# A two-layer decoder trunk: index scores of the sparse attention summed over the heads on TensorE with diagonal operands, in place of multiply-and-add steps on VectorE

## The chip, the cores and the metric

The kernel runs on one core of a Trainium2 chip. The metric is the device time of one execution in microseconds (us); the time before is the median of three runs. The profile is of one further execution, with its own time. TensorE (PE, with its weight loads PEld) multiplies matrices and writes only to PSUM; VectorE (DVE), ScalarE (ACT) and GpSimd (POOL) work elementwise; SyncE (SP) issues the DMAs here. Each engine takes its instructions in the order in which the program holds them.

## The reference

The model has two layers. Layer 0 runs two groups of heads in parallel on 256 tokens of width 1024: A, a sliding-window attention, and B, a sparse attention in which an indexer picks 64 keys per query. Layer 1 is a block attention. After each attention and each MLP stands a residual with a layer norm, and every step is modulated by factors from a conditioning vector `c` (the "ada" products). The change touches the indexer of B only:

```python
def one_block(args):
    i, qb, iqb, iwb = args                       # 128 queries, 8 index heads of 64
    raw = jnp.einsum('bqhd,bsd->bhqs', iqb, ik)  # index scores of each head
    score = jnp.einsum('bhqs,bqh->bqs', jax.nn.relu(raw), iwb)   # weighted sum over the 8 heads
    score = jnp.where(causal, score, -inf)
    _, idx = lax.top_k(score, 64)                # S // 4 keys of each query
    ...                                          # softmax attention over the picked keys
```

For each query the eight heads' scores pass through a ReLU, are multiplied by eight weights of that query (`iw`), and are added up. The largest 64 of the sum select the keys.

## The kernel before

The 256 tokens are two blocks of 128 (b = 0 and 1), tokens on the partitions. Block 0 sees 128 keys, block 1 sees 256. All is float32; large weight matrices are split by ACT (L170) and DVE (L171) into a high and a low part, and each product is three matmuls (L236 to L238).

The order of the program comes from a scheduler: code is emitted in an order written out by hand (the strings of steps at L887 and L954, generators that are advanced in turn), each instruction gets a priority from its place, shifted by a few tuned offsets (L46), and the scheduler sets the final order on each engine. Buffers are rings of tiles: `wh` and `wl` (six each) hold split weights, `q4`, `r2`, `prob` and so on the activations; PSUM has four rings (`a` to `d`) of two banks. Reuse of a ring's tile waits for the last reader of what it held.

The stage around the change, by the lines that the prediction names:

- L661 and L681 project the tokens; L715 copies the result `g0` out of PSUM. From it come the keys, the latent queries and the weights `iw` (L765). L736 to L741 normalise the latent queries: DVE sums the squares, POOL computes the power -1/2 (L302), DVE scales (L741), TensorE transposes (L744) and ACT copies (L746).
- L784 makes queries of them, a pair of matmuls for each of four query sets (index queries of both blocks, attention queries of both blocks). Each is rotated by DVE (L471 to L475, `rope`), transposed (L491) and copied by ACT (L493).
- `index(b)`: for each pair of heads, two matmuls of 128 queries by 128 or 256 keys (L817), one ReLU by ACT out of PSUM into `rl` (L819), and for each head one DVE instruction (L822) that multiplies by the head's weight of each query and adds to `score`; the first adds to the causal mask.
- `select(b)` then takes the largest eight (L833) and strikes them out (L834), eight times, and makes a mask (L837, L838).
- Beside this runs group A's attention in half steps: two score matmuls (L531), mask and maximum on DVE (L535), exponentials on ACT (L539), transposes (L545), products with the values (L553).
- Into each half step one "ada" product is placed on TensorE: eight matmuls on a loaded weight tile (L347), a copy by ACT (L357), two matmuls with one column (L368), and an addition on DVE (L377). A fixed chain holds these, L531, L545 and L553 in turn on TensorE. L347 needs a PSUM bank that an earlier L377 has read.
- SP loads the weights into a ring of four raw tiles (L164). A tile's successor is issued when its tile has been read.
- L410 and L417 spread a gate vector over the partitions; L608 uses it in the residual after the output projection (`ps_out`). Then follow the first MLP, layer 1 and the second MLP, which are nearly all dense matmuls.

Of the kernel before, what the change touches and what calls it, by code (L numbers as in the profile page):

```python
# [17 lines left out]
F32 = mybir.dt.float32  # L18
# [3 lines left out]
AF = mybir.ActivationFunctionType  # L22
ALU = mybir.AluOpType

P = 128
D = 1024
KT = 8
NB = 2
# [36 lines left out]
def trunk(ctx: ExitStack, tc, c, x, pos, small, ln, ada, w_g, w_g1, w_uq, w_out, c_in, c_out, w1, w2, out):  # L65
    nc = tc.nc
    const = ctx.enter_context(tc.tile_pool(name="const", bufs=1))
    wp = ctx.enter_context(tc.tile_pool(name="wp", bufs=NRAW))
    sp = ctx.enter_context(tc.tile_pool(name="sp", bufs=NSPLIT))
    hp = ctx.enter_context(tc.tile_pool(name="hp", bufs=1))  # L70
    work = ctx.enter_context(tc.tile_pool(name="work", bufs=1))
    psum = ctx.enter_context(tc.tile_pool(name="psum", bufs=1, space=bass.MemoryType.PSUM))

    def pa(name):
        return psum.tile([P, 512], F32, name=name, tag="a", bufs=2)

    def pb(name):
        return psum.tile([P, 512], F32, name=name, tag="b", bufs=2)

    def pc(name):  # L80
        return psum.tile([P, 512], F32, name=name, tag="c", bufs=2)
# [173 lines left out]
    for b in range(NB):  # L255
        t = const.tile([P, D], F32, name=f"x{b}")
# [10 lines left out]
    for h in range(2):  # L267
        ps = pa("ps_c")
# [7 lines left out]
    ident = const.tile([P, P], F32, name="ident")  # L276
# [335 lines left out]
    def moments(st):  # L612
        mv = col([P, 2], "mv")
        nc.vector.bn_aggr(mv, st.rearrange("p a s -> p (a s)"))
        rs = col([P, 1], "rs")
        nc.vector.tensor_scalar_add(rs, mv[:, 1:2], LN_EPS)
        rsqrt(rs, rs)
        return mv, rs
# [44 lines left out]
    for k in range(KT):  # L663
# [16 lines left out]
        for b in range(NB):  # L680
            nc.tensor.matmul(g1[b], hk[:, b * P:(b + 1) * P], parts["g1", k // 2][0][:, k % 2 * 512:k % 2 * 512 + 512],  # L681
                             start=k == 0, stop=k == KT - 1)
# [3 lines left out]
    m = nc.vector.tensor_copy(posf, posi)  # L686
# [40 lines left out]
    iw = work.tile([P, NB, 8], F32, name="iw")  # L727
# [4 lines left out]
    for b in range(NB):  # L732
        t = g0[b]
# [3 lines left out]
                                       op0=ALU.mult, op1=ALU.add, accum_out=ss)  # L737
# [4 lines left out]
        ps = pc("ps_cq")  # L742
# [5 lines left out]
    for b in range(NB):  # L748

        t = g0[b]  # L750
        q = slice(b * P, (b + 1) * P)
# [3 lines left out]
        ps = pc("ps_kd")  # L755
# [8 lines left out]
        nc.gpsimd.tensor_copy(vB[:, b, :64], t[:, 320:384])  # L764
        nc.vector.tensor_scalar_mul(iw[:, b], t[:, 448:456], IW_SCALE)  # L765

    def q4(name):
        return work.tile([P, 4, 256], F32, name=name, tag="q4", bufs=5)

    def to_qT(qf, dst, b):  # L770
# [3 lines left out]
             [(d[:, :, b * P:(b + 1) * P], slice(i * n, (i + 1) * n)) for i, d in enumerate(dst)])  # L774

    iqT, aqT = q4("iqT"), q4("aqT")
    bqT = work.tile([P, 1040], F32, name="bqT", tag="vv", bufs=2)[:, :1024].rearrange("p (n q) -> p n q", n=4)
    hf = lambda t: t.rearrange("p (h q) d -> p h q d", h=2)
# [28 lines left out]
    def index(b):  # L807
        nk = P * (b + 1)
        m = mC[:, P:] if b == 0 else mC
        sc = work.tile([P, 256], F32, name="score", tag="prob2", bufs=2)  # L810
        first = True
        for p0 in (0, 2):
            for half in range(2):
                ps = pb("ps_i")
                rl = work.tile([P, 2, 256], F32, name="rl", tag="prob", bufs=3)
                for j in range(2):
                    nc.tensor.matmul(ps[:, j * 256:j * 256 + nk], iqT[:, p0 + j, b * P:(b + 1) * P],  # L817
                                     ikT[half][:, :nk], start=True, stop=True)
                nc.scalar.activation(rl[:, :, :nk], ps.rearrange("p (j k) -> p j k", j=2)[:, :, :nk], AF.Relu)  # L819
                for j in range(2):  # L820
                    hd = 2 * (p0 + j) + half
                    nc.vector.scalar_tensor_tensor(sc[:, :nk], in0=rl[:, j, :nk], scalar=iw[:, b, hd:hd + 1],  # L822
                                                   in1=(m if first else sc[:, :nk]), op0=ALU.mult, op1=ALU.add)
                    first = False
        return sc

    def select(b, sc):
# [28 lines left out]
    def index_keys(b):  # L856
        scores[b] = index(b)
# [194 lines left out]
    def c_project(g, got):  # L1052
        qT = q4("cqT_")

        kT = [q4("ckT_"), work.tile([P, 4 + 2 * g, 256], F32, name="ckT_", tag=("pair", "keys")[g])[:, :4]]
        for half in range(2):
            nc.gpsimd.memset(kT[half][(1 - half) * HD:(2 - half) * HD], 0.0)
        vv = work.tile([P, 1040], F32, name="vv", tag="vv", bufs=2)
        vv = vv.rearrange("p (b h e) -> p b h e", b=NB, h=8)
        got += [qT, kT, vv]  # L1060
        nc.gpsimd.memset(vv[:, :, :, 64:], 1.0)

        def products(part, b):
            ps = pa("ps_c")
            project(ps, hT, b, [("ci", 6 * g + 2 * part), ("ci", 6 * g + 2 * part + 1)])
            if part == 2:
                nc.scalar.copy(vv[:, b, :, :64], heads_of(ps))
            else:
                b_rope(ps, ([qT], kT)[part], b)

        for part, b in ([(0, 0), (1, 0), (0, 1), (1, 1)] if g == 0 else [(0, 0), (0, 1), (1, 0), (1, 1)]) + [(2, 0), (2, 1)]:
            products(part, b)
            if b == 1:
                ahead(1)
            if g == 0 and (part, b) != (0, 0):
                for _ in range(2):
                    next(more, None)
            yield
# [33 lines left out]
    first = moments(zs[0][1])  # L1112
# [4 lines left out]
    for s in halves:  # L1117
        z = zs[1][0]
        nc.vector.scalar_tensor_tensor(z[:, s], in0=z[:, s], scalar=mv[:, 0:1], in1=gb[0][:, s],  # L1119
                                       op0=ALU.subtract, op1=ALU.mult)  # L1120
# [55 lines left out]
```

## Time and profile before

| | |
|---|---|
| median of three runs | 667.27 us (663.51 to 668.79) |
| profiled execution, its time | 670.48 us |
| its span, first to last instruction | 668.7 us |
| PE / DVE / ACT / POOL busy | 636.8 / 470.5 / 339.4 / 34.1 us |
| mean granted TensorE clock | 0.976 |
| L822, first and last start | 60.4 and 79.1 us |

The profile gives times from the start of the span. Where rows of one kind follow each other, a group stands as its first start, the time to its last end, and a count; a float32 matmul of 128 or 256 columns is recorded as two rows, so "x4" is two matmuls. Ends of matmuls are modelled, so the time that one costs is read from start to next start. In brackets stands how long an engine was idle before a row, and what ended that.

### The profile page before, as it was taken

The page shows a single profiled execution, that of the slowest core. Times are in us where ns is not written, and L with a number is a line of the kernel's source. Part 1 is how long each engine was busy: PE and PEld are TensorE (multiplying, and loading weights), DVE is VectorE, ACT ScalarE, POOL GpSimd, SP SyncE. Part 2 cuts the span into 40 slices and gives each one's busy share as a digit, 9 for nine tenths or more (in the row PEclk, how much of TensorE's full clock was granted, in tenths as well). Part 3 has the DMA queues.
Part 4 walks back from the last instruction along what each step waited for, and adds up shares of the span by engine and source line. Part 5 has one row for each costly group of instructions (what it writes and reads, how often), then busy time and mean ns, then how long its engine had stood idle before and what let it go on. Part 6 is the DMA issues. An engine that isn't in the chain of part 4 may idle for free. (4 is left out here: it accounts for less than half of the span.)

```text
span 668.7 us, 9851 instructions
## 1 busy us (share of the span) xinstructions
PE 636.8 (95%) x3802; PEld 533.1 (80%) x3802; DVE 470.5 (70%) x885; ACT 339.4 (51%) x540; POOL 34.1 (5%) x69
## 2 busy tenths in 40 slices
PE   6998998989999999999989999999999999999994
PEld 3554776868899998989867888888899989898983
DVE  2848987348778989888796996755867755554447
ACT  3325657436645445445544555873654554545440
POOL 5010000100010000200010000000000000000004
PEclk8999989989999999999979999999999999999997
DMA  8993879233679897899742486311467755565101
GB/s 305 409 414 114 298 272 350 95 126 125 239 270 368 328 370 272 330 362 370 273 179 101 159 356 223 137 72 63 143 235 256 296 204 190 197 235 195 67 1 63
DMA packets 24385, 151.52 MB, mean 227 GB/s; under 512 B 2833, under 2 KB 3089, under 8 KB 8338
## 3 DMA queue, kind: packets, MB, share of 16 engines
q1 hardware_dynamic: 24194, 150.71, 60.9%
q8 instruction: 30, 0.49, 0.3%
q10 hardware_dynamic: 144, 0.18, 0.1%
q14 instruction: 17, 0.14, 0.1%
HBM read 149.83 MB, written 1.05 MB: 226 GB/s over the span
## 5 line engine op out<-in xcount | busy, mean ns | idle before, releaser
L170 ACT CAST wh<-w_w 128x1024 fp32r<-128x1024 f32 x128 | 130.9, 1051 | 152.8 <-PE ps_m L237 66.6
L171 DVE TENSOR_TENSOR wl<-w_w,wh 128x1024 fp32r<-128x1024 f32 x128 | 153.4, 1222 | 70.5 <-ACT wh L170 70.3
L236 PE MATMUL ps_m<-hTh,wh 128*128 128x256 f32 x448 | 126.8, 283 | 0.0
L238 PE MATMUL ps_m<-hTh,wl 128*128 128x256 f32 x448 | 126.7, 283 | 0.0
L237 PE MATMUL ps_m<-hTl,wh 128*128 128x256 f32 x448 | 126.6, 283 | 0.0
L238 PE MATMUL ps_m<-wh,ul 128*128 128x512 f32 x256 | 101.4, 397 | 0.6 <-DVE ul L171 0.6
L236 PE MATMUL ps_m<-wh,uh 128*128 128x512 f32 x256 | 101.1, 398 | 0.0
L237 PE MATMUL ps_m<-wl,uh 128*128 128x512 f32 x256 | 100.8, 395 | 0.0
L322 DVE CUSTOM_DVE_ANT_0 junk<-w_ada,cB,sm 128x1024 bf16<-128x1024 f32 x68 | 87.1, 1282 | 15.1 <-DMA w_ada<-in_ada_dram 13.6
L237 PEld LDWEIGHTS ps_m<-hTl,wh 128*128 128x128 f32 x448 | 85.7, 191 | 1.3
L236 PEld LDWEIGHTS ps_m<-hTh,wh 128*128 128x128 f32 x448 | 85.7, 191 | 1.2
L238 PEld LDWEIGHTS ps_m<-hTh,wl 128*128 128x128 f32 x448 | 85.8, 191 | 0.0
L238 PEld LDWEIGHTS ps_m<-wh,ul 128*128 128x128 f32 x256 | 48.2, 188 | 12.2 <-DVE ul L171 1.2
L236 PEld LDWEIGHTS ps_m<-wh,uh 128*128 128x128 f32 x256 | 48.3, 189 | 10.2 <-ACT uh L170 0.6
L237 PEld LDWEIGHTS ps_m<-wl,uh 128*128 128x128 f32 x256 | 48.2, 188 | 9.7 <-DVE wl L171 0.2
L236 PE MATMUL ps_c<-wh,hTh 128*128 128x512 f32 x96 | 39.6, 416 | 2.8 <-ACT hTh L170 2.0
L237 PE MATMUL ps_c<-wl,hTh 128*128 128x512 f32 x96 | 39.0, 408 | 0.0
L238 PE MATMUL ps_c<-wh,hTl 128*128 128x512 f32 x96 | 38.6, 402 | 0.0
L171 DVE TENSOR_TENSOR ul<-relu,uh 128x512 fp32r<-128x512 f32 (+1 forms) x36 | 22.6, 627 | 17.5 <-ACT uh L170 17.5
L539 ACT ACTIVATE prob<-prob,negm 128x128 f32<-128x128 f32 (+1 forms) x64 | 26.8, 452 | 14.8 <-DVE negm L535 14.8
L171 DVE TENSOR_TENSOR wl<-w_ci,wh 128x1024 fp32r<-128x1024 f32 x24 | 28.6, 1213 | 5.3 <-ACT wh L170 5.2
L170 ACT CAST wh<-w_ci 128x1024 fp32r<-128x1024 f32 x24 | 24.8, 1051 | 11.8 <-PE ps_c L238 5.6
(231 smaller groups left out, 994.6 us busy)
## 6 DMA issues: line engine op xcount, KB each, us to landing
w_w<-in_w_dram SPq DMA_DIRECT2D x64, 1024.0 KB, 5.0
w_ada<-in_ada_dram SPq DMA_DIRECT2D x40, 1024.0 KB, 7.0
w_ci<-in_c_in_dram SPq DMA_DIRECT2D x12, 1024.0 KB, 5.0
w_ada<-in_ada_dram SPq DMA_DIRECT2D x12, 512.0 KB, 9.5
w_wo<-in_w_out_dram SPq DMA_DIRECT2D x4, 1024.0 KB, 5.1
w_co<-in_c_out_dram SPq DMA_DIRECT2D x4, 1024.0 KB, 4.9
w_g<-in_w_g_dram SPq DMA_DIRECT2D x8, 356.0 KB, 9.1
early<-in_ada_dram SPq DMA_DIRECT2D x4, 512.0 KB, 8.5
```

The lines of the kernel that those rows point to most:

```text
L170: nc.scalar.copy(dh, src)
L171: return nc.vector.tensor_sub(dl, src, dh.bitcast(F32))
L236: nc.tensor.matmul(ps, a[0], b[0], start=start, stop=False)
L237: nc.tensor.matmul(ps, a[0], b[1], start=False, stop=False)
L238: nc.tensor.matmul(ps, a[1], b[0], start=False, stop=stop)
L322: state[key, j] = nc.vector.tensor_tensor_reduce(out=junk, in0=w, in1=cB, scale=1.0, scalar=bias, op0=ALU.mult, op1=ALU.add, accum_out=m)
L539: state["exp"] = nc.scalar.activation(pr[:, j, :nk], pr[:, j, :nk], AF.Exp, bias=negm[:, hd:hd + 1], scale=-1.0)
```

## The change

The eight weights of each query are written, by POOL, as eight diagonal matrices of 128 by 128 per block (the identity times a column of `iw`, L771 of the new file), into a tile of the `wl` ring. The ReLU results of all eight heads are kept in two tiles of the `wh` ring, ordered by head. Eight float32 matmuls (L830 of the new file) multiply each head's scores by its diagonal and accumulate in one PSUM bank of ring `c`; one DVE addition (L831) puts the causal mask on and writes `score`. The sixteen DVE instructions of L822 go, and `rl` leaves the `prob` ring. In the new file L784 has become L793, L802 L811, L817 L825, L819 L827, and L833, L834 are L840, L841.

```diff
+    def head_weights(b):
+
+        t = sp.tile([P, 1024], F32, name="diag", tag="wl").rearrange("p (h q) -> p h q", h=8)
+        for hd in range(8):
+            nc.gpsimd.tensor_scalar(t[:, hd], ident, iw[:, b, hd:hd + 1], None, op0=ALU.mult)
+        return t
+
+    diag = [head_weights(b) for b in range(NB)]
+
...
         sc = work.tile([P, 256], F32, name="score", tag="prob2", bufs=2)
-        first = True
+        rl = [sp.tile([P, 1024], F32, name="rl", tag="wh").rearrange("p (h k) -> p h k", h=4) for _ in range(2)]
         for p0 in (0, 2):
             for half in range(2):
                 ps = pb("ps_i")
-                rl = work.tile([P, 2, 256], F32, name="rl", tag="prob", bufs=3)
                 for j in range(2):
                     nc.tensor.matmul(ps[:, j * 256:j * 256 + nk], iqT[:, p0 + j, b * P:(b + 1) * P],
                                      ikT[half][:, :nk], start=True, stop=True)
-                nc.scalar.activation(rl[:, :, :nk], ps.rearrange("p (j k) -> p j k", j=2)[:, :, :nk], AF.Relu)
-                for j in range(2):
-                    hd = 2 * (p0 + j) + half
-                    nc.vector.scalar_tensor_tensor(sc[:, :nk], in0=rl[:, j, :nk], scalar=iw[:, b, hd:hd + 1],
-                                                   in1=(m if first else sc[:, :nk]), op0=ALU.mult, op1=ALU.add)
-                    first = False
+                nc.scalar.activation(rl[p0 // 2][:, half:half + 3:2, :nk], ps.rearrange("p (j k) -> p j k", j=2)[:, :, :nk], AF.Relu)
+        ps = pc("ps_is")
+        for hd in range(8):
+            nc.tensor.matmul(ps[:, :nk], diag[b][:, hd], rl[hd // 4][:, hd % 4, :nk], start=hd == 0, stop=hd == 7)
+        nc.vector.tensor_add(sc[:, :nk], ps[:, :nk], m)
```

The scheduler places the new instructions, and moves some old ones. The first place is POOL, after the projection, as a piece of the difference (+ is new; `ss` is the sum of squares of a block, first of block 0, then of block 1):

```order
 L764 COPY vB<-g_357 128x64
+L771 TENSOR_SCALAR diag<-ident,iw 128x128
 L302 TENSOR_TENSOR ss<-ss,mhalf 128x1
+L771 TENSOR_SCALAR diag<-ident,iw 128x128 x7
 L764 COPY vB<-g_357 128x64
+L771 TENSOR_SCALAR diag<-ident,iw 128x128
 L302 TENSOR_TENSOR ss<-ss,mhalf 128x1
```

The second power of L302 stands behind nine new instructions, one of them ahead of the first power too. The other seven of block 1 come after it.

The second place is TensorE at the index of block 0, where `ps_uq` are the query matmuls and `qr` the rotated queries. Before:

```order
L817 MATMUL ps_i<-keys,iqT 128x128 x4
L784 MATMUL ps_uq<-w_uq,pair 128x512
L347 MATMUL ps_ada<-w_ada_8_287,cT 32x256 x8
L491 MATMUL ps_T<-ident,qr 128x128 x4
L817 MATMUL ps_i<-keys,iqT 128x128 x2
L531 MATMUL ps_s<-keys,aqT 128x128 x2
L491 MATMUL ps_T<-ident,qr 128x128 x4
L545 MATMUL ps_pt<-ident,prob 128x128 x2
```

And now:

```order
L825 MATMUL ps_i<-keys,iqT 128x128 x3
L347 MATMUL ps_ada<-w_ada_8_287,cT 32x256 x8
L825 MATMUL ps_i<-keys,iqT 128x128 x2
L491 MATMUL ps_T<-ident,qr 128x128
L825 MATMUL ps_i<-keys,iqT 128x128
L491 MATMUL ps_T<-ident,qr 128x128 x3
L793 MATMUL ps_uq<-w_uq,pair 128x512
L531 MATMUL ps_s<-keys,aqT 128x128 x2
L491 MATMUL ps_T<-ident,qr 128x128
L830 MATMUL ps_is<-rl,diag 128x128 x8
L491 MATMUL ps_T<-ident,qr 128x128 x3
L545 MATMUL ps_pt<-ident,prob 128x128 x2
```

The last query matmul moved from ahead of the ada product to behind it, all index matmuls and the first four transposes; the eight new matmuls stand inside the second group of transposes.

The third place is TensorE at the index of block 1. Before:

```order
L347 MATMUL ps_ada<-w_ada_10_315,cT 32x256 x8
L817 MATMUL ps_i<-keys,iqT 128x256 x6
L531 MATMUL ps_s<-keys,aqT 128x128 x2
L545 MATMUL ps_pt<-ident,prob 128x128 x2
L553 MATMUL ps_pv<-vA,probT 128x65 x2
L368 MATMUL ps_ada<-four,adarows 128x1 x2
L347 MATMUL ps_ada<-w_ada_11_360,cT 32x256 x8
```

And now:

```order
L347 MATMUL ps_ada<-w_ada_10_315,cT 32x256 x8
L825 MATMUL ps_i<-keys,iqT 128x256 x5
L830 MATMUL ps_is<-rl,diag 128x256 x8
L531 MATMUL ps_s<-keys,aqT 128x128 x2
L545 MATMUL ps_pt<-ident,prob 128x128 x2
L553 MATMUL ps_pv<-vA,probT 128x65 x2
L368 MATMUL ps_ada<-four,adarows 128x1 x2
L347 MATMUL ps_ada<-w_ada_11_360,cT 32x256 x8
```

The eight new matmuls of 256 columns stand between the index matmuls and the next half step of group A. Farther on, L410 and the first five L417 stand behind the first output-projection matmuls instead of ahead of them; from the first matmul of the first MLP on, the order of every engine is as before.

## The prediction

> **What bounds the kernel now.** I read the page's first part, then busy time by stretches (columns: length, then busy time and count for PE, PEld, DVE, ACT and POOL, then the granted clock, the DMA share and GB/s), cut where the index stage begins and ends on TensorE and where the output projection begins.
>
> ```profile
> PE 636.8 (95%) x3802; PEld 533.1 (80%) x3802; DVE 470.5 (70%) x885; ACT 339.4 (51%) x540; POOL 34.1 (5%) x69
> 52.00:79.18 27.18, 23.60 (x165) 15.85 (x165) 25.56 (x84) 16.70 (x43) 0.00 (x0) 1.00 0.50 186
> 79.18:118.59 39.41, 36.30 (x323) 27.71 (x323) 30.75 (x129) 24.71 (x55) 0.97 (x5) 0.91 0.84 309
> ```
>
> Over the whole span TensorE is the busy engine. In the index stage, 52.00 to 79.18, DVE is the fuller one (25.56 of 27.18 us), yet PE is busy for 23.60: it stands idle for only 3.58 us. From 79.18 on PE is ahead again. So the stage is close to balanced, and what moves work from DVE to PE can earn at most PE's idle time there. What ended that idle time, between 52 and 119 us:
>
> ```profile
> PE ps_ada L347 <- DMA w_ada<-in_ada_dram: 1.8, 1, 1.8
> PE ps_T L491 <- DVE qr L475: 1.4, 2, 1.1
> PE ps_ada L347 <- DVE mod L377: 1.2, 1, 1.2
> ```
>
> The two DVE rows, 2.6 us, are all that DVE costs PE in this stage. The DMA row stands later, at 111.64.
>
> **The change, part by part.** *Removed: sixteen L822 on DVE.* Two groups by form (count, busy time, mean ns, idle time before), then rows in order of time (start, length), as in all that follow:
>
> ```profile
> L822 DVE SCALAR_TENSOR_TENSOR score<-rl,iw,score 128x256 f32<-128x256 f32 x7 | 3.3, 474 | 0.0
> L822 DVE SCALAR_TENSOR_TENSOR score<-rl,iw,score 128x128 f32<-128x128 f32 x7 | 2.4, 347 | 0.9 <-ACT rl L819 0.9
> ...
> 63.36 0.68 DVE L471 TENSOR_TENSOR rope<-ps_uq,cosT 128x512 f32<-128x512 f32 x1
> ...
> 65.63 0.35 DVE L822 SCALAR_TENSOR_TENSOR score<-rl,iw,score 128x128 f32<-128x128 f32 x1 [0.39 <-ACT rl L819]
> 65.89 0.69 DVE L475 TENSOR_TENSOR qr<-rope,rope 128x512 f32<-128x512 f32 x1
> ...
> 78.58 0.48 DVE L822 SCALAR_TENSOR_TENSOR score<-rl,iw,score 128x256 f32<-128x256 f32 x1
> 78.97 0.15 DVE L377 TENSOR_TENSOR mod<-ps_ada,sm 128x2 f32<-128x2 f32 x1
> ```
>
> From start to next start one takes 0.26 (128 keys) or 0.39 (256 keys): 8 x 0.26 + 8 x 0.39 = 5.2 us. Two additions L831 come in; the nearest row is the mask addition L838, though it reads SBUF and not PSUM:
>
> ```profile
> 100.08 0.43 DVE L838 TENSOR_TENSOR pair<-score,mC 128x256 f32<-128x256 f32 x1
> ```
>
> At most 0.43 each, 0.9 in all, so DVE is relieved of at least 4.3 us. For PE that is worth no more than the 2.6 us of waits above.
>
> *Added: sixteen L830 on PE.* They have the shape of the index matmuls L817: a 128x128 float32 stationary operand, 128 or 256 moving columns.
>
> ```profile
> 61.13 1.06 PE L817 MATMUL ps_i<-keys,iqT 128*128 128x128 f32 x8
> 62.02 1.02 PE L784 MATMUL ps_uq<-w_uq,pair 128*128 128x512 f32 x2
> 62.98 1.07 PE L347 MATMUL ps_ada<-w_ada,cT 128*32 128x256 f32 x16
> ...
> 73.27 3.23 PE L817 MATMUL ps_i<-keys,iqT 128*128 128x256 f32 x12
> 76.34 0.61 PE L531 MATMUL ps_s<-keys,aqT 128*128 128x128 f32 x4
> ...
> 79.18 1.07 PE L347 MATMUL ps_ada<-w_ada,cT 128*32 128x256 f32 x16 [1.23 <-DVE mod L377]
> ```
>
> Four of 128 columns take 0.89 us to the next start, 0.22 each; six of 256 take 3.07, 0.51 each. 8 x 0.22 + 8 x 0.51 = 5.9 us on PE, all in its queue ahead of the 39 us stretch in which PE is the bound. That already exceeds the 3.58 us of idle time: had PE no wait left in the stage, it would still end 5.9 - 3.6 = 2.3 us later.
>
> *The place of block 0.* PE waited here for the last rotated queries:
>
> ```profile
> 66.64 0.66 PE L491 MATMUL ps_T<-ident,qr 128*128 128x128 f32 x4 [1.11 <-DVE qr L475]
> 67.13 0.38 PE L545 MATMUL ps_pt<-ident,prob 128*128 128x128 f32 x2
> ```
>
> One would expect DVE, without its first eight L822, to bring these 2 to 3 us sooner. But the order moves the last query matmul (62.02 before, 0.96 to the next start) behind the ada product (1.0, the row at 62.98), two more index matmuls (0.44) and four transposes (0.49, the rows above): it starts at 62.02 + 1.93 = 63.95 and ends at 64.9. Its rotation can't begin before. That took 3.28 us from L471 at 63.36 to PE's start at 66.64; three of the L822 between (0.8) and the wait of 0.39 go, and one L535 comes, which I take at an L822's 0.3: 2.4 us. So the queries come at 64.9 + 2.4 = 67.3, against 66.6. DVE's relief buys nothing here; the wait ends 0.6 us later. The bank that L830 fills is read by L831 only after DVE's next rotation steps, and L545 needs that bank: 0 to 0.4 us more, which I leave to the range.
>
> *The place of block 1.* Before, L347 waited 1.23 us for L377, which stood on DVE behind L822. Now L830 runs ahead of that half step, DVE has only L831 and two L535 there, and L377 waits for L368 alone. The nearest row for that:
>
> ```profile
> 92.80 1.07 PE L347 MATMUL ps_ada<-w_ada,cT 128*32 128x256 f32 x16 [0.23 <-PE ps_ada L368]
> ```
>
> So 1.23 falls to about 0.2: -1.0. A small wait at 70.71 (the other 0.3 of the 1.4) goes too: -0.3.
>
> *Added: sixteen L771 on POOL.* No row has this form. From below stands a cast of the same 128x128; from above a two-input product of 128x352 beside DVE work, per element:
>
> ```profile
> 1.61 0.28 POOL L281 CAST identb<-ident 128x128 bf16<-128x128 f32 x1
> 662.67 1.06 POOL L1104 TENSOR_TENSOR x<-z,lngB 128x352 f32<-128x352 f32 x1
> ...
> 44.81 0.42 DVE L736 CUSTOM_DVE_ANT_0 junk<-g 128x256 bf16<-128x256 f32 x1 [4.79 <-ACT g L715]
> 44.84 0.49 POOL L764 COPY vB<-g 128x64 f32<-128x64 f32 x1 [35.49 <-ACT g L715]
> ...
> 45.52 0.57 POOL L302 TENSOR_TENSOR ss<-ss,mhalf 128x1 f32<-128x1 f32 x1 [0.19 <-DVE ss L738]
> 48.00 0.55 POOL L302 TENSOR_TENSOR ss<-ss,mhalf 128x1 f32<-128x1 f32 x1 [0.18 <-DVE ss L738]
> 48.59 0.35 DVE L741 TENSOR_SCALAR cqn<-g,ss 128x256 f32<-128x256 f32 x1 [0.67 <-POOL ss L302]
> 50.20 0.23 DVE L800 COPY vA<-evac 128x128 f32<-128x128 f32 x1 [0.78 <-ACT evac L481]
> 52.14 0.29 DVE L471 TENSOR_TENSOR rope<-evac,cosT 128x128 f32<-128x128 f32 x1 [0.30 <-PE ps_kd L757]
> ```
>
> 0.28 at least; 1.06 x 128/352 = 0.39 by elements alone, and up to 0.6 if half of the 1.06 is fixed. I take 0.3, nearest to the cast, which also has one input. The second L302 then starts not at 48.00 but after 45.5 + 0.3 + 0.6 (first L302) + 7 x 0.3 + 0.5 (copy) + 0.3 = 49.3, with 0.2 for contention 49.5: L741 of block 1, and all of DVE behind it, is 1.5 us late. DVE's own pauses at 50.20 and 52.14, 1.1 us, take that up but for 0.4. The transposes of block 0 don't wait for it, and ACT was held until 50.3 by copies. So +0.4 (from 0, to 52.0 - 48.0 - 1.1 = 2.9 at 0.6 each). The rest of L771 is done by about 52, long before L830 needs it.
>
> The first power and the copy on POOL read the same memory as L736: the copy of 64 elements took 0.49 beside it, more than the 0.28 of a cast of 128 alone. The Trainium skill (SBUF — State Buffer, Who interferes with whom) says that a DVE instruction with two SBUF inputs and a GpSimd instruction that reads SBUF exclude each other for a whole instruction; the 0.49 agrees, and by that rule the L771 would be held up by L736 at times, and DVE by them.
>
> *Moved, at no cost.* The last query matmul frees the raw tile of `w_uq`, so the weight loads behind it on SP leave about 1.9 us later:
>
> ```profile
> 63.08 0.33 SPq L164 DMA_DIRECT2D w_ada<-in_ada_dram  x1
> 64.11 0.33 SPq L164 DMA_DIRECT2D w_wo<-in_w_out_dram  x1
> 72.12 1.06 ACT L170 CAST hTh<-w_wo 128x1024 fp32r<-128x1024 f32 x1
> w_wo<-in_w_out_dram SPq DMA_DIRECT2D x4, 1024.0 KB, 5.1
> ```
>
> Landing at 65.0 + 5.1 = 70.1 they are there before 72.12. ACT now has this cast ahead of the copies of keys and queries of block 1, which would stall with it; PE reaches their readers at about 72, so without this cover it would cost up to 1 us. The gate's L417 go behind the projection's matmuls, which end near 124; the first residual that reads the gate stands at 132.27:
>
> ```profile
> 132.27 0.69 DVE L608 TENSOR_TENSOR z<-ps_out,gateB 128x512 f32<-128x512 f32 x1 [1.93 <-PE ps_out L238]
> ```
>
> The `wh` and `wl` rings shift by whole pairs, so a split waits for a tile as old as before. ACT's eight ReLUs stay.
>
> Sum: +5.9 + 0.6 - 1.0 - 0.3 + 0.4 = **+5.6 us** at the start of the 39 us stretch, where PE carries it to the end.
>
> **The clock.** One thing could give part back. Granted clock after the 1.23 us wait:
>
> ```profile
> 77.00:80.40 3.40, 2.17 (x27) 1.51 (x26) 3.40 (x19) 1.92 (x6) 0.00 (x0) 1.00 0.97 378
> 80.50:83.90 3.40, 3.40 (x18) 2.99 (x18) 2.77 (x16) 1.36 (x4) 0.00 (x0) 0.50 0.75 229
> 83.90:87.20 3.30, 3.30 (x21) 1.76 (x21) 1.68 (x6) 0.37 (x1) 0.00 (x0) 0.50 0.51 129
> ```
>
> After 3.4 us in which PE was busy for 2.17, the clock is halved for 6.7 us: up to 6.7 x 0.5 = 3.3 us lost. With L830 packed in ahead and the wait gone, I expect no dip there: -3.3 against an execution that had it. By the Trainium skill (TensorE: Matmul & The Clock Gate, Part 1) the clock halves after an idle window of about 3.4 us, free-running. The length of the dip, two such windows, agrees; the idleness doesn't, since PE was idle for at most 1.23 us at a stretch here. By the page a run without such a gap would have no dip before or after, and the sum would be the plain +5.6.
>
> **How the numbers follow.** The profiled execution took 670.48 us (span 668.7 and 1.8 around it); the median of the runs is 667.27, 3.2 less, about the size of one dip. Without the dip, the profiled execution becomes 670.5 + 5.6 - 3.3 = 672.8. From the median: 667.3 + 5.6 = 672.9 if it had no dip, 667.3 + 2.3 = 669.6 if it had one. I take the middle, **671.2 us**, 0.6% above 667.27.
>
> **The rivals.** *The clock dips elsewhere.* PE's wait for the queries of block 0 grows from 1.1 to 2.0 us (65.3, when two score matmuls at 0.22 are done, to 67.3). Before, the 1.11 there cost no clock, and the 1.23 at 79 did. If it tips: 672.9 + 3.3 = 676.2 at most. Chance 0.15; slower by over 1%.
>
> *POOL becomes the gate.* At 0.6 us for an L771, the second power starts at about 52, DVE is 2.9 us late rather than 0.4: 672.9 + 2.5 = 675.4; the order of POOL speaks for it, the 0.28 cast against. It decides from 0.5 us each. Chance 0.12.
>
> *DVE's relief comes through (not slower).* All of PE's 3.58 us of waits go, and the dip with them: 667.3 + 5.9 - 3.6 - 3.3 = 666.3. For it speaks DVE's 25.56 of 27.18; against it, the moved query matmul. It decides if PE is busy without pause from 59 to 84. Chance 0.18. That the change leaves the time as it is, because the added matmuls fit in waits, is the same case.
>
> The forecast has 0.55. The runs of before spread by some 2.5 us to either side, and I count 1% as what a measurement tells from no change: faster under 660.6, slower over 673.9. Slower: 0.15 + 0.08 of the POOL case + 0.03 of the forecast's upper edge = 0.26. Faster needs 5.7 us more than this last case, and later waits such as the DMA's 1.8 keep their place: 0.04. The range reaches from the third rival, 666.5, to the first, 676.
>
> **What would show it.** Right: L830 at 0.22 and 0.51 us each, L302 of block 1 starting near 49.5, the last query matmul near 64, L347 of the next ada product after block 1's index about 5 us later than 79.18 (near 84), and equal spacing from there to the output projection. Wrong: L771 above 0.5 us, L830 cheaper than L817, a dip in other windows, or DVE idle where I have it working to 67.

## The result and the profile after

| | before | after |
|---|---|---|
| median of the runs | 665.40 us (663.51 to 668.79, 4 runs) | 673.82 us (673.19 to 675.55, 4 runs) |
| profiled execution, its time | 670.48 us | 673.19 us |
| its span | 668.7 us | 671.4 us |
| mean granted TensorE clock in it | 0.976 | 0.983 |

The changed kernel takes 1.0126 times as long, 95% interval 1.0089 to 1.0163: 1.3% slower, 8.4 us on the medians.

The busy times of the page of the changed kernel say little, as those of before did: PE has 1.7 us more, DVE 2.7 us less, POOL 9.0 us more.

```profile
PE 638.5 (95%) x3834; PEld 536.3 (80%) x3834; DVE 467.8 (70%) x871; ACT 339.5 (51%) x540; POOL 43.1 (6%) x85
```

Those 9 us of POOL are where to look first. GpSimd's instructions of the changed kernel in order of time (start, length, then the row as before):

```profile
43.70 0.49 POOL L764 COPY vB<-g 128x64 f32<-128x64 f32 x1 [34.34 <-ACT g L715]
44.38 0.61 POOL L771 TENSOR_SCALAR diag<-ident,iw 128x128 f32<-128x128 f32 x1 [0.19 <-issue]
44.96 0.56 POOL L302 TENSOR_TENSOR ss<-ss,mhalf 128x1 f32<-128x1 f32 x1
45.52 4.37 POOL L771 TENSOR_SCALAR diag<-ident,iw 128x128 f32<-128x128 f32 x7
49.83 0.24 POOL L764 COPY vB<-g 128x64 f32<-128x64 f32 x1
50.04 0.60 POOL L771 TENSOR_SCALAR diag<-ident,iw 128x128 f32<-128x128 f32 x1
50.61 0.57 POOL L302 TENSOR_TENSOR ss<-ss,mhalf 128x1 f32<-128x1 f32 x1
51.17 4.85 POOL L771 TENSOR_SCALAR diag<-ident,iw 128x128 f32<-128x128 f32 x7
```

One L771 takes 0.61 to 0.62 us (seven in 4.37; the last seven, in 4.85, take 0.69 each), and not the 0.3 of the forecast. Eight of them stand between the two powers L302, and POOL runs from 44.38 to 50.61 without a pause before it comes to the second. What this does to DVE and PE stands in their rows of the changed kernel, in order of time:

```profile
43.67 0.42 DVE L736 CUSTOM_DVE_ANT_0 junk<-g 128x256 bf16<-128x256 f32 x1 [3.66 <-ACT g L715]
...
51.21 0.46 DVE L741 TENSOR_SCALAR cqn<-g,ss 128x256 f32<-128x256 f32 x1 [4.39 <-POOL ss L302]
51.82 0.66 PE L744 MATMUL ps_cq<-ident,cqn 128*128 128x128 f32 x2 [3.48 <-DVE cqn L741]
...
67.95 1.02 PE L793 MATMUL ps_uq<-w_uq,pair 128*128 128x512 f32 x2
69.01 0.69 DVE L471 TENSOR_TENSOR rope<-ps_uq,cosT 128x512 f32<-128x512 f32 x1 [3.64 <-PE ps_uq L793]
71.29 0.33 PE L491 MATMUL ps_T<-ident,qr 128*128 128x128 f32 x1 [1.87 <-DVE qr L475]
71.46 1.96 PE L830 MATMUL ps_is<-rl,diag 128*128 128x128 f32 x16
73.25 0.49 PE L491 MATMUL ps_T<-ident,qr 128*128 128x128 f32 x3
...
82.46 3.62 PE L830 MATMUL ps_is<-rl,diag 128*128 128x256 f32 x16
85.91 0.61 PE L531 MATMUL ps_s<-keys,aqT 128*128 128x128 f32 x4
86.11 0.42 DVE L831 TENSOR_TENSOR score<-ps_is,mC 128x256 f32<-128x256 f32 x1 [2.86 <-PE ps_is L830]
...
87.45 1.07 PE L347 MATMUL ps_ada<-w_ada,cT 128*32 128x256 f32 x16
```

DVE, which was to be relieved, stands idle three times in these rows: 4.39 us for POOL, 3.64 us for the last query matmul (67.95) and 2.86 us for the added sums. PE waits 3.48 us for L741, and this wait did not exist before. The last row is the mark by which the kernels are compared below: the ada product behind block 1's index, counted from the first L736 (43.67 here). That is 43.78 us; before, 79.18 - 44.81 = 34.37. So the stage has become 9.4 us longer.

The clock after that wait, in windows of the changed kernel (length, busy time and count of PE, PEld, DVE, ACT and POOL, then the granted clock, the DMA share and GB/s):

```profile
50.00:52.00 2.00, 0.18 (x1) 0.21 (x2) 0.79 (x4) 0.00 (x0) 2.00 (x5) 0.77 0.98 395
52.00:54.00 2.00, 2.00 (x5) 0.86 (x5) 1.97 (x11) 0.62 (x2) 2.00 (x3) 0.50 0.25 98
54.00:56.00 2.00, 2.00 (x5) 0.98 (x4) 1.31 (x5) 1.04 (x4) 2.00 (x4) 0.50 0.01 2
56.00:58.00 2.00, 2.00 (x6) 1.31 (x5) 1.97 (x5) 1.15 (x5) 0.02 (x1) 0.52 0.00 0
```

The dip is not gone: it stands at the new wait and not near 80 any more. By the mean clock of the first and the last window it lasts from 51.1 to 57.9, that is 6.8 us. TensorE's waits of the changed kernel from 44 to 122 us, with the time in all, the number and the longest:

```profile
PE ps_cq L744 <- DVE cqn L741: 3.5, 1, 3.5
PE ps_ada L347 <- DMA w_ada<-in_ada_dram: 2.0, 1, 2.0
PE ps_T L491 <- DVE qr L475: 1.9, 1, 1.9
```

The wait of 1.23 us for L377 is gone, the one for the rotated queries has grown from 1.11 to 1.87, and the one for the weights has stayed (1.8 before, 2.0 now).

### The profile page after: what moved, and what is told of

It is laid out like the page before. It is cut to its first block, busy times and chain, and to the rows that moved or that the text cites. A ratio compares the mean times of both kernels' runs of the same rounds, so it can differ in the third digit from the quotient of the medians.

```text
span 671.4 us, 9912 instructions
## 1 busy us (share of the span) xinstructions
PE 638.5 (95%) x3834; PEld 536.3 (80%) x3834; DVE 467.8 (70%) x871; ACT 339.5 (51%) x540; POOL 43.1 (6%) x85
## 5 line engine op out<-in xcount | busy, mean ns | idle before, releaser
L170 ACT CAST wh<-w_ci 128x1024 fp32r<-128x1024 f32 x24 | 24.8, 1051 | 12.3 <-PE ps_c L238 5.5
```

The source lines that it names most:

```text
L170: nc.scalar.copy(dh, src)
```

## The experiments

The first theory was that three terms add up: GpSimd's order (the diagonals ahead of the second power), TensorE's order (the last query matmul behind the ada product), and the sixteen matmuls themselves. The rival was that one of them alone is the bound and hides the others. A second question was what the dip of the clock is worth. All kernels are compared with the kernel before on the same chip: 663.63 us (21 runs) beside the first four experiments, 664.96 us (23 runs) beside the last three.

The marks of all kernels, in us from the first L736 of the same execution; "time" is the difference of the medians from before:

| kernel | L741 of block 1 | last rotation L471 | L347 behind block 1's index | longer than before by | time | ratio (95% interval) |
|---|---|---|---|---|---|---|
| before | 3.78 | 18.55 | 34.37 | | | |
| after | 7.54 | 25.34 | 43.78 | 9.4 | +8.4 | 1.0126 (1.0089 to 1.0163) |
| after, again | 7.55 | 24.05 | 42.48 | 8.1 | +7.9 | 1.0102 (1.0065 to 1.0139) |
| powers first | 3.78 | 20.75 | 39.19 | 4.8 | +7.1 | 1.0088 (1.0054 to 1.0122) |
| queries first | 7.54 | 21.96 | 40.15 | 5.8 | +4.3 | 1.0067 (1.0041 to 1.0094) |
| both first | 3.77 | 18.67 | 36.85 | 2.5 | +2.5 | 1.0029 (1.0003 to 1.0055) |
| both first, one-pass sum | 3.77 | 18.67 | 34.11 | -0.3 | -1.3 | 0.9971 (0.9942 to 0.9999) |
| before, with diagonals only | 7.55 | 23.34 | 39.15 | 4.8 | +5.5 | 1.0086 (1.0051 to 1.0121) |
| after, with filler | 7.62 | 24.44 | 42.77 | 8.4 | +10.8 | 1.0147 (1.0100 to 1.0194) |

The marks of a row come from one profiled execution, the times from all runs. In the kernels with an edit to the order of the queries the lines stand two further down (L736 is L738, L795 is the query matmul, L832 the sum).

### The powers ahead of the diagonals

```diff
-            nc.gpsimd.tensor_scalar(t[:, hd], ident, iw[:, b, hd:hd + 1], None, op0=ALU.mult)
+            behind("pow", nc.gpsimd.tensor_scalar(t[:, hd], ident, iw[:, b, hd:hd + 1], None, op0=ALU.mult))
```

The order of the other engines is that of the changed kernel.

> The changed kernel, with all sixteen diagonal products on POOL tied behind the second power of the normalisation; every other engine keeps the changed kernel's order. Theory A (POOL's queue is what went wrong: the diagonal products held the second power, PE waited 3.5 us for it, and the clock was halved for 6.9 us after that): both go, 673.8 - 3.5 - 3.4 = about 667, and no stretch at half clock between 50 and 58 us. Theory B (the loss is the sixteen added matmuls on TensorE): 672 to 674, since they are all still there.

Measured: 670.72 us (668.35 to 671.60, 7 runs). GpSimd, DVE and PE in this kernel:

```profile
44.98 0.42 DVE L736 CUSTOM_DVE_ANT_0 junk<-g 128x256 bf16<-128x256 f32 x1 [4.50 <-ACT g L715]
...
48.17 0.55 POOL L302 TENSOR_TENSOR ss<-ss,mhalf 128x1 f32<-128x1 f32 x1 [0.18 <-DVE ss L738]
48.71 11.48 POOL L771 TENSOR_SCALAR diag<-ident,iw 128x128 f32<-128x128 f32 x16
48.76 0.46 DVE L741 TENSOR_SCALAR cqn<-g,ss 128x256 f32<-128x256 f32 x1 [0.67 <-POOL ss L302]
...
84.17 1.07 PE L347 MATMUL ps_ada<-w_ada,cT 128*32 128x256 f32 x16
```

The second power waits for DVE again, as before the change, and L741 stands at 3.78 us from the mark. The stage is 3.3 us shorter than in the repeated run of the changed kernel (42.48 to 39.19). The time lies between the two expectations, nearer to the second: 2.2 to 3.1 us below the changed kernel's as the medians stand, 0.9 to 1.3 if each is taken against the runs of before beside it. GpSimd's order is a term of the loss, and not the larger part of it.

### The diagonals alone, unused

The kernel before, with POOL writing the sixteen diagonals and nothing reading them; L822 stays on DVE.

```diff
+    def head_weights(b):
...
+    diag = [head_weights(b) for b in range(NB)]
```

> The kernel before, with the sixteen diagonal products added on POOL and read by nobody; scores are summed on VectorE as before. Theory A: POOL's queue alone costs nearly the whole difference, 665.4 + 3.5 + 3.4 = about 672, with the wait for the second block's normalised queries and the half clock at 50 to 58 us. Theory B: 665 to 667, nothing on TensorE was added.

Measured: 669.18 us (666.54 to 673.30, 9 runs), again between the two expectations. Its rows:

```profile
43.99 0.42 DVE L736 CUSTOM_DVE_ANT_0 junk<-g 128x256 bf16<-128x256 f32 x1 [3.42 <-ACT g L715]
...
51.54 0.47 DVE L741 TENSOR_SCALAR cqn<-g,ss 128x256 f32<-128x256 f32 x1 [4.39 <-POOL ss L302]
52.15 0.66 PE L744 MATMUL ps_cq<-ident,cqn 128*128 128x128 f32 x2 [3.49 <-DVE cqn L741]
...
83.14 1.07 PE L347 MATMUL ps_ada<-w_ada,cT 128*32 128x256 f32 x16 [1.22 <-DVE mod L377]
```

Without one of the new matmuls there stands the whole wait of 3.49 us, and the stage is 4.8 us longer. The wait comes from GpSimd alone. These 4.8 us hold a dip of 6.8 us at the wait as well. The 1.22 us for L377 is still there; it is gone only in the kernels without L822.

### The last query matmul back in its place, with the powers first

```diff
-            in_turn(nc.tensor.matmul(ps[g, :256], cT[:, k:k + 1].to_broadcast([P, 32]),
-                                     w[:, 256 * k:256 * (k + 1)], start=k < 4, stop=k >= 4))
+            m = nc.tensor.matmul(ps[g, :256], cT[:, k:k + 1].to_broadcast([P, 32]),
+                                 w[:, 256 * k:256 * (k + 1)], start=k < 4, stop=k >= 4)
+            behind("uq", m)
+            in_turn(m)
```

`state["uq"]` is the last query matmul.

> As the kernel with the powers first, and the last query matmul also tied ahead of the first ada product, where the kernel before had it. If that moved matmul is what kept VectorE's relief from TensorE (wait of 1.9 us at the transposes of block 0, VectorE idle 3.6 us before it), the wait goes and the time is about 2 us below the kernel with the powers first, some 665. If the relief is hidden elsewhere, the time is the same as there, 667.

Measured: 666.16 us (664.18 to 669.44, 12 runs), 4.6 us less than with the powers first alone, and so more than the place of the query matmul was expected to be worth. In the trace:

```profile
43.23 0.42 DVE L738 CUSTOM_DVE_ANT_0 junk<-g 128x256 bf16<-128x256 f32 x1 [3.69 <-ACT g L717]
...
53.98 0.63 PE L493 MATMUL ps_T<-ident,qr 128*128 128x128 f32 x4 [0.26 <-DVE qr L477]
...
61.90 0.69 DVE L473 TENSOR_TENSOR rope<-ps_uq,cosT 128x512 f32<-128x512 f32 x1 [1.56 <-PE ps_uq L795]
...
74.22 0.59 PE L832 MATMUL ps_is<-rl,diag 128*128 128x256 f32 x2
74.65 1.03 PE L827 MATMUL ps_i<-keys,iqT 128*128 128x256 f32 x4
75.52 3.19 PE L832 MATMUL ps_is<-rl,diag 128*128 128x256 f32 x14
78.54 0.61 PE L533 MATMUL ps_s<-keys,aqT 128*128 128x128 f32 x4
...
80.08 1.07 PE L347 MATMUL ps_ada<-w_ada,cT 128*32 128x256 f32 x16
```

DVE's wait for the last query matmul falls from 3.64 to 1.56, and of PE's waits for rotated queries one of 0.26 us is left. The edit moves more than the query matmul: the scheduler also orders anew, around it, some masks and rotations of DVE and some copies of ACT, so what follows is the worth of that whole order. The stage is 2.5 us longer than before. Here DVE's relief does come through, and it is spent: PE's three waits for DVE of before, 1.11, 0.28 and 1.23 us, are gone but for 0.26, and 5.2 us of matmuls less these 2.4 make 2.8. That the prediction's floor, 5.9 - 3.6 = 2.3, lies so near is luck: the 5.9 was too high, and the 3.6 holds a wait of 0.77 us for ACT that has stayed.

### The four orders together

The changed kernel again on this chip, and the changed kernel with only the query matmul put back (the edit just shown, without the one on GpSimd, and with the new order on DVE and ACT that comes with it):

> The changed kernel as it is, beside the others of this group, so that the two orders (powers ahead of the diagonals on GpSimd, last query matmul ahead of the first ada product on TensorE) can be compared in all four combinations on one chip. From its four runs so far: 673 to 675 us. Theory A (the two orders and the added matmuls are separate terms that add up): 673.8. Theory B (they are one chain in which only the later of the two counts): the same here; it differs in the next kernel.

> The changed kernel with only the query matmul put back ahead of the first ada product; the diagonals still stand between the two powers on GpSimd. Theory A (the two orders add up): the moved query matmul is worth 4.6 us with the powers first (670.7 to 666.2), and the same here: 669.2. Theory B (one chain: with the second power 3.8 us late, VectorE is late anyway, and the place of the query matmul behind the ada product costs little): 672 to 674. In its trace the product L347 behind block 1's index then comes about 41.5 us (A) or 43 us (B) after VectorE's first L736, against 43.8 in the changed kernel and 39.2 with the powers first.

Measured: 672.90 us (670.60 to 674.68, 6 runs) and 669.29 us (668.11 to 672.87, 12 runs). The sum of the terms was expected to give 669.2. The mark of the product L347 in the four kernels:

| | diagonals between the powers | powers first | difference |
|---|---|---|---|
| query matmul behind the ada product | 42.48 | 39.19 | 3.29 |
| query matmul first | 40.15 | 36.85 | 3.30 |
| difference | 2.33 | 2.34 | |

In the stage the two terms add up to the hundredth, so neither hides the other. (Both executions of the left column had a dip of 3.4 us behind GpSimd's wait. With the first execution of the changed kernel, whose dip was 6.8 us long, 43.78 stands in place of 42.48, and two of the differences become 4.59 and 3.63.) The rival of one chain is out: the delay of L741 is carried by PE through all that follows, and so is the delay of the last rotation. In time the split is less clean: the query matmul is worth 3.6 and 4.6 us, more than its 2.3, and GpSimd's order 2.2 and 3.1, or 0.9 and 1.8 against the runs of before beside each, less than its 3.3. Together they are worth 6.7 us, or 5.4 so compared, against 5.6 in the stage.

The rest of the program shows why. From the mark L347 to the end of the span, in the profiled executions ("half clock" is added up from the granted clock in windows of 2 us; the last column is PE's longest wait for an ada weight between 90 and 126 us):

| kernel | L347 to the end | of it at half clock | less half of that | wait for the weight |
|---|---|---|---|---|
| before | 589.52 | 25.0 | 577.0 | 1.76 |
| after | 583.95 | 12.8 | 577.6 | 1.99 |
| after, again | 582.97 | 12.8 | 576.6 | none |
| powers first | 585.63 | 16.0 | 577.6 | 2.57 |
| queries first | 581.54 | 9.1 | 577.0 | 0.88 |
| both first | 582.82 | 8.2 | 578.7 | 2.96 |
| both first, one-pass sum | 583.39 | 12.3 | 577.2 | 0.69 |
| before, with diagonals only | 584.56 | 12.6 | 578.3 | 1.91 |
| after, with filler | 582.24 | 9.0 | 577.7 | 0.85 |

Without half of the time at half clock the rest is the same within 2.1 us in all nine, and part of that goes with the wait for the weight. So the dips that an execution happens to have there make most of what the stage doesn't explain. The runs without a profile have no such windows, but they have a mean clock: its medians are 0.9845 (after, again), 0.985 (powers first), 0.986 (queries first) and 0.988 (both first). An estimate from these: at half clock a kernel loses 1 - clock of its time, 10.4, 10.0, 9.4 and 8.0 us, of which 1.7 belong to the stage's own dip in the first and the third, if all their runs had it. Without the rest of that loss the query matmul is worth 2.6 and 2.5 us and GpSimd's order, taken between two chips, 3.5 and 3.4, close to the 2.3 and 3.3 of the stage.

### The sum in one pass

Both orders as above, and diagonals and ReLU results in fp32r, so that the sum over the heads is taken at a lower precision.

```diff
-        t = sp.tile([P, 1024], F32, name="diag", tag="wl").rearrange("p (h q) -> p h q", h=8)
+        t = sp.tile([P, 1024], F32R, name="diag", tag="wl").rearrange("p (h q) -> p h q", h=8)
...
-        rl = [sp.tile([P, 1024], F32, name="rl", tag="wh").rearrange("p (h k) -> p h k", h=4) for _ in range(2)]
+        rl = [sp.tile([P, 1024], F32R, name="rl", tag="wh").rearrange("p (h k) -> p h k", h=4) for _ in range(2)]
```

> Both orders as in the best kernel so far (666.2 us), and the sixteen matmuls L830 read their diagonals and their relu tiles as fp32r, the type of the projections' split operands, so that the index sum is taken at a lower precision. The fp32r matmuls of the projections follow each other at 0.233 us for 512 columns; by that 256 columns take 0.12 instead of 0.43 and 128 columns at most the 0.22 they take now. Theory A (what is left over before is the time of the sixteen matmuls on TensorE): 8 x 0.31 = 2.5 us less at least, 3.8 at most: 662.4 to 663.7, at or below the kernel before. Theory B (what is left is something else, the weight load for the ada product at 110 us or VectorE's order): 665.5 to 666.5.

Measured: 663.69 us (660.84 to 664.98, 12 runs), 2.5 us less than with float32 as the medians stand, 3.8 against the runs of before beside each, within what the first theory expected. The matmuls of this kernel are recorded as one row each:

```profile
65.29 1.08 PE L832 MATMUL ps_is<-rl,diag 128*128 128x128 f32 x8
66.21 0.40 PE L547 MATMUL ps_pt<-ident,prob 128*128 128x128 f32 x2
...
75.03 0.82 PE L832 MATMUL ps_is<-rl,diag 128*128 128x256 f32 x4
75.69 0.38 PE L533 MATMUL ps_s<-keys,aqT 128*128 128x128 f32 x2
...
77.91 1.07 PE L347 MATMUL ps_ada<-w_ada,cT 128*32 128x256 f32 x16
```

From start to next start one costs 0.115 us (128 columns), against 0.22. The four of 256 columns take 0.66 us to the next start, but 0.31 of that passes behind the first of them; those that follow each other directly stand 0.12 us apart, as expected, against 0.43. In the stage that makes 36.85 - 34.11 = 2.7 us, more than the 2.5 that were left. So what was left is the time of the matmuls in float32 on PE. The ratio to before is 0.9971, with an interval that ends just below one: level with the kernel before or a little faster, at the price of precision in the sum that picks the keys.

### Filler in the wait

```diff
+        for _ in range(8 * b):
+            nc.tensor.matmul(ps[:, 256:], ident, cB[:, :256], start=True, stop=True)
```

Eight matmuls that compute nothing needed, in an unused half of the bank that L744 writes, run while PE waits for L741 of block 1. (In this file they are L744, and the transposes are L746.)

> The changed kernel, with eight float32 matmuls of 256 columns on TensorE (3.4 us, into an unused half of the bank, read by nobody) placed in the 3.5 us wait for the second block's normalised queries. The wait for POOL stays. If the half clock after that wait comes from TensorE's idleness, it goes: 673.8 - 3.4 = about 670.5, although work was added. If it comes at its own time, or the wait alone is the loss: 673.8 or a little more.

Measured: 674.40 us (669.19 to 676.31, 6 runs). Rows and windows of its trace:

```profile
49.00 3.62 PE L744 MATMUL ps_cq<-cB,ident 128*128 128x256 f32 x16
...
58.37 0.63 PE L491 MATMUL ps_T<-ident,qr 128*128 128x128 f32 x4 [1.18 <-DVE qr L475]
```

```profile
52.00:54.00 2.00, 1.24 (x7) 0.60 (x7) 1.89 (x9) 0.63 (x2) 2.00 (x4) 1.00 0.21 82
54.00:56.00 2.00, 1.43 (x6) 0.46 (x4) 1.90 (x10) 1.56 (x6) 2.00 (x4) 1.00 0.00 0
56.00:58.00 2.00, 1.16 (x3) 0.36 (x3) 1.90 (x4) 1.04 (x4) 1.39 (x2) 1.00 0.00 0
```

The filler fills the wait, 49.00 to 52.62, and the dip is gone. The expectation tied two things together, and only the first came: the dip goes when PE has work in the wait, but the time doesn't fall. The stage is not shorter either: 42.77 us, against 42.48 in the repeated run of the changed kernel, which was at half clock there for 3.4 us. DVE starts the block's work 3.8 us late with or without the dip, and PE then waits for it, 1.18 us at a place where the changed kernel, slowed by the clock, doesn't. This suggests that the dip is mostly hidden behind DVE, but it is not shown: the edit also made the scheduler put a pair of query matmuls (0.86 us to the next start) behind these transposes instead of ahead of them, which can make most of that wait by itself. What a longer dip costs is seen between the two executions of the changed kernel: half clock for 6.8 us and for 3.4 us, marks at 43.78 and 42.48, so 1.3 us for 3.4 us more at half clock. The kernel with the diagonals alone had the long dip too: 3.3 us for GpSimd's order and 1.3 for the longer dip make 4.6 of its 4.8. The runs of the filler kernel differ by their clock: two at 0.991 and 0.993 took 669.19 and 671.25 us, the other four, at 0.983 to 0.988, 674.14 to 676.31.

## Why the prediction was right or wrong

The time, 673.82, came out inside the range of 666.5 to 676.0 and 2.6 us above the predicted one. It lies 0.98% above the 667.27 known then, and 1.26% above the median of before with one more run. The change itself was forecast at +3.9 us (671.2 - 667.27) and measured +8.4, so it was half as large in the forecast as in fact.

**Sixteen L830 on PE, 5.9 us: right in kind, a little high.** They take 0.22 and 0.43 us from start to next start (16 rows in 1.79 and 3.45 us), 5.2 us in all. The price for 256 columns, 0.51 from six L817, was too high by 0.08 each. With it the sum without GpSimd would be 4.5 us.

**The place of block 0, +0.6: right.** The last query matmul is moved, its rotation can't begin before, and PE's wait for the rotated queries is 1.87 us where 2.0 was worked out. What the step left out is what the place is worth against the place that could have been had: 2.3 us in the stage, since without L822 and with the query matmul ahead this wait is 0 and not the 1.11 of before.

**The place of block 1, -1.0, and the small wait, -0.3: right.** Both are gone.

**These four terms together** gave 5.2 us without GpSimd. With the powers first the stage is 4.8 us longer. Its last query matmul starts at 64.67 and L347 at 84.17, which in before's time is 64.5 and 84.0; the prediction had them near 64 and near 84.

**L771 at 0.3 each, +0.4 us: this is the step that failed.** It was priced by a cast of the same size (0.28) and measured 0.61. The rival "POOL becomes the gate", with 0.12, had the right price and the right consequence: it had the second power at about 52 and DVE 2.9 us late, and measured was 51.75 in before's time (50.61, in an execution that began the stage 1.14 us earlier) and 3.3 us in the stage. The forecast's sum had 0.4 of that. The row from above was nearer, 1.06 us for a product of 352 columns: with half of it fixed it gives 0.53 + 0.53 x 128/352 = 0.72, and not the 0.6 that the prediction worked out, and 0.61 lies between that and the 0.39 by elements alone. The prediction had named an L771 above 0.5 us as a sign of being wrong; it came.

**The pauses of DVE at 50.20 and 52.14 that were to take up the delay** did not: the delay of 3.8 us at L741 came through as 3.3 us. The block's transposes and query matmuls wait for L741 too, so PE itself stood for 3.48 us.

**The clock, -3.3: wrong in its base and in its place.** The dip at 80 is gone as forecast, but the wait for POOL brings one at 51. And the execution that was profiled before was no typical one: its mean clock was 0.976, while the median of 21 later runs of the same kernel is 0.989. Behind the stage it was at half clock for 25.0 us, the eight other executions for 8.2 to 16.0; the dip at 80 is 6.8 of that. The price of half the dip's length fits where PE is the bound, as the table of the rest shows. The middle between "with" and "without" was taken from 667.27; in groups of 21 and 23 runs the median of before is 663.63 and 664.96. That base was 2 to 4 us too high and made up for most of the mis-sized term, which is luck: the time was met better than the change was.

**The rival of the clock that dips elsewhere** came as well, at another wait than it named. Its price there was not isolated: the 1.3 us between two executions, for 3.4 us more at half clock, is all that the runs show, and the kernel with the filler gains nothing without the dip.

**DVE's relief comes through:** not in the changed kernel, but in the one with both orders put right, where of PE's waits for DVE 0.26 us is left. Of the 3.58 us that this rival let go, only the 2.6 of the two DVE rows could go.

**Moved at no cost:** the loads of `w_ada` and `w_wo` left later (66.87 and 69.01), the cast behind them waited 0.20 us, and PE's wait for weights is 2.0 where it was 1.8; that cover held. The gate's L417 cost nothing: the first residual that reads the gate waits 1.91 us for its matmul, as it did (1.93).

## What to carry to other kernels

When work is taken off a busy engine, ask of each engine that takes it up what stands behind it in its queue: an instruction that nobody needs for 20 us, put ahead of a 0.55 us power, held up DVE and PE. An operation without a row of its own is to be priced by the upper row as well as the lower, and where one of the two would make it a gate, the order of that queue matters more than the price. A stage in which PE has 3.6 us of idle time can't be made shorter by 5 us of added matmuls, whatever they relieve; here it took both orders and a cheaper form of matmul to come out even. And before a difference of 1% in the time is put down to a stage, the rest of the program is to be compared as well: here the dips of the clock in it differed by up to 17 us at half clock from one execution to another.

## What the runs showed of the hardware

A multiplication of a 128x128 float32 tile by one value for each partition took 0.61 us on GpSimd with DVE idle, twice the 0.28 us of a cast of that size to bf16. Beside DVE's rotations it took 0.72 (sixteen in 11.48 us), and DVE's L741 took 0.46 in place of 0.35 us while such a row ran. The Trainium skill (SBUF — State Buffer, Who interferes with whom) has a DVE instruction with two SBUF inputs, or in a mode that takes both ports, and a GpSimd instruction that reads SBUF block each other for a whole instruction. The rows agree in direction, with a mean loss of 0.1 us for each; which of DVE's instructions are of these two kinds, no run here shows.

All four executions in which PE waited 3.48 us at this place (3.49 in one) went to half clock there (after, its repetition, queries first, diagonals only); none of the five without that wait did (before, powers first, both first, its one-pass form, filler). A window of the kernel with the diagonals alone, then three of the repeated run of the changed kernel:

```profile
50.00:52.00 2.00, 0.00 (x0) 0.00 (x0) 0.46 (x2) 0.14 (x1) 2.00 (x5) 0.74 1.00 404
...
54.00:56.00 2.00, 1.69 (x4) 0.73 (x5) 2.00 (x12) 0.62 (x2) 2.00 (x4) 0.66 0.05 18
56.00:58.00 2.00, 2.00 (x5) 0.99 (x4) 1.57 (x7) 1.04 (x4) 2.00 (x4) 0.50 0.00 0
58.00:60.00 2.00, 2.00 (x8) 0.95 (x7) 1.97 (x5) 1.32 (x6) 1.07 (x1) 0.99 0.00 0
```

By the mean clock of its window the dip with the diagonals alone begins at 51.0, while PE still stands: its wait began at 48.7 and ended at 52.15. The same holds for the changed kernel (dip from 51.1, wait from 48.3 to 51.8). So 2.3 and 2.7 us of idleness were enough, and these two dips lasted 6.8 us. In the repeated run and with the queries first the dip begins 0.3 us behind the wait's end and lasts 3.4 us.

The Trainium skill (TensorE: Matmul & The Clock Gate, Part 1) puts an idle window of about 3.4 us ahead of the half clock, free-running. The dips' lengths, one and two such windows, agree, and so does it that the dips begin at different points against the wait. The idleness doesn't: 2.3 us is less than a whole window. The dip of before at 80, behind a wait of 1.23 us, speaks the same way. But with the same wait of 1.22 us the kernel with the diagonals alone had no dip, and a wait of 2.96 us for weights (to 110.38, both first) was followed by none while one of 2.57 us (to 114.07, powers first) was. So the length of a wait alone doesn't decide; what else does stays open.
